# Roots pinned behind the last tanh, mLSTM sums in column groups, and keys and values spread by two rounded products

## The chip, the cores and the metric

The kernel runs on one core of a Trainium2 chip. The core has a matrix engine (TensorE, in the profile PE, with its weight loads as PEld), VectorE (DVE), ScalarE (ACT), GpSimd (POOL) and the engine that issues most DMAs (SP). Each engine takes its own instructions in order and waits on semaphores for the others. Matrix products land in PSUM, eight banks of 128 x 512 fp32; everything else lies in SBUF. The metric is the time of one execution in microseconds (us); lower is better.

## What is computed

One step of a recurrent decoder layer, for a prompt of 256 tokens and for 8 sequences of 4 new tokens, side by side: 288 columns. Three branches share one input product, their results are merged by sigmoid gates, and an MLP follows. Cut to what the change touches:

```python
proj = xn @ P['w_in']                      # then split into the branches
# RG-LRU
a = jnp.exp(log_a)
u = jnp.sqrt(-jnp.expm1(2.0 * log_a)) * (i * x)        # the roots
h = a_t * h + u_t                                      # scan over tokens
# GLA and mLSTM, for each new sequence: state update with keys and values
S = jnp.exp(bL)[..., None] * S + jnp.einsum('bhjd,bhje->bhde', k_ * jnp.exp(bL - b), v_)
C = cs[..., None, None] * C + jnp.einsum('bhj,bhjd,bhje->bhde', wj, k_, v_)
# mLSTM
S = jnp.einsum('bhid,bhjd->bhij', q_, k_) * W
den = ci * jnp.einsum('bhid,bhd->bhi', q_, n) + jnp.sum(S, axis=-1)   # the sums
# output gate of GLA
y_gla = rmsnorm(o) * jax.nn.silu(g_gate)               # the gate tanh
```

## The kernel before

**Streams.** All arrays are held with features on the 128 partitions and the 288 columns (N) free. Weights come from memory in tiles of 512 KB. `halve` (line 155 and on) splits each tile into a rounded part `hi` (ScalarE, line 164, to the type fp32r) and the remainder `lo` (VectorE, line 171). `stream_` then makes three fp32r products for each pair of a weight block and an input block (lines 197 to 199), four output blocks at a time, each in its own PSUM bank of the pool `pm` (4 banks). When a bank has its last product, `evac` empties it. A step of a stream is one weight tile: 2 x 4 x 3 = 24 products.

**Side work.** The branches' own arithmetic is written as generators (`lru`, `gla`, `gates`, `mlstm`) that `run` advances by one `yield` for each step of a stream, so that it fills the other engines while TensorE streams. The side's products take PSUM from `misc()` (pool `px`, 2 banks) or `longp()`. `run` gives them high priority and has them issued behind the current step's last product, `lo` and `hi` (`issue_after`). Within that, the order on TensorE, VectorE, ScalarE and GpSimd is made when the program is built, by a simulated run that places what is ready first; only SP's order is written out by hand. `issue_after(x)` demands a place behind x on an engine's queue; it isn't a wait.

**The roots.** `lru` starts beside the last input stage, and its 19th call falls on the first step of the merge gates, behind the two blocks of output gates (`B_GATE`). There it takes four square roots (line 759). `gate_silu` evicts a gate block: a tanh on ScalarE (line 837) and a multiply-add on VectorE (line 838). ScalarE has to load a table of functions when it goes from tanh to square root and back (ACT_TABLE_LOAD).

**The sums.** In the head loop of `mlstm`, w0 and w1 hold the weighted scores of a head for two blocks of 128 keys (256 and 128 queries wide); they lie in `e0`, in one of two places in turn. Lines 1436 and 1437 multiply them by a full 128 x 128 block of ones, which gives the sum over keys in every output row, and line 1438 copies 32 of these rows into `den`.

**Keys and values.** The new tokens' keys and values lie with (head, token) on the partitions. For the state updates they have to be spread over partitions, with a rounded part in some rows and the remainder in others, so that one fp32r product carries both. `copies` builds a selector of zeros and ones by GpSimd copies of the identity (line 862), `parts` multiplies by it in fp32 (line 876), rounds the product into `dst` (line 877), and then, with the column pairs `K_LO` and `V_LO`, turns the remainder rows into product minus rounded product (lines 881 and 882). `by_half` and `spread` follow, then `update`. The calls: `first` and `second` in `gla`, `part` in `mlstm`; 128 columns for GLA's keys, 256 for its values and for both in mLSTM. In `gla` the selector lies in slot 9, in `mlstm` in slot 4; the tile that the values later use (slot 4 in `gla`, slot 2 in `mlstm`) is taken only behind it.

Of the kernel before, what the change touches and what calls it, by code (L numbers as in the profile page):

```python
# [8 lines left out]
F32 = mybir.dt.float32  # L9
F32R = mybir.dt.float32r  # L10
# [4 lines left out]
P = 128  # L15
# [11 lines left out]
NPRE = 6  # L27


CONSTS = [("ident", 128), ("eye", 32), ("seq", 4), ("ends", 8), ("klo", 2), ("vlo", 2), ("smask", 32), ("slo", 32),  # L30
          ("glo", 128), ("causal", 128), ("bdm", 128), ("hsel", 4), ("head", 4), ("half", 2)]
PARAMS = [("bada", 96), ("g1", 16), ("lcw", 32), ("lcb", 8), ("mcw", 32), ("mcb", 8), ("ba", 8), ("bx", 8), ("lam", 8),
# [21 lines left out]
def trunk(ctx, tc, io):  # L54
# [678 lines left out]
    def lru():  # L733
        wax = slot(3)
        wa = flat(wax)[:, 0:1024].rearrange("p (n d) -> p n d", n=8)
        wx = flat(wax)[:, 1024:2048].rearrange("p (n d) -> p n d", n=8)
        G.dma_start(flat(wax)[:, 0:2048], io["lruw"])
        uc = slot(4)
        yield
        yield from conv(lx, uc, Pm("lcw"), Pm("lcb"), "lst", "o_lconv", slot(1), True)  # L740
        ls2, ls4, hb = rates
        thr, thi, tt = slot(5), slot(0), slot(1)
        aa = thr
        ps = {}
        for n in range(8 + 2):
            if n >= 2:
                i = n - 2
                for j, t in ((0, thr), (1, thi)):
                    S.activation(t[:, i, :], ps.pop((i, j))[:, :N], AF.Tanh, bias=hb[:, j, i:i + 1], scale=0.5)
                S.activation(tt[:, i, :], thr[:, i, :], AF.Tanh, bias=ls2[:, i:i + 1], scale=ls2[:, i:i + 1])  # L750
                exp = S.activation(aa[:, i, :], thr[:, i, :], AF.Exp, bias=ls4[:, i:i + 1], scale=ls4[:, i:i + 1])
            if n < 8:
                for j, w in ((0, wa), (1, wx)):
                    ps[n, j] = misc()
                    T.matmul(ps[n, j][:, :N], w[:, n, :], uc[:, n, :], start=True, stop=True)  # L755
            yield
        with tc.issue_after(exp.ins):
            for h in range(4):
                S.activation(tt[:, 2 * h:2 * h + 2], tt[:, 2 * h:2 * h + 2], AF.Sqrt, scale=-0.25)
        for h in range(4):  # L760
            r = slice(2 * h, 2 * h + 2)
            V.scalar_tensor_tensor(thi[:, r], thi[:, r], 1.0, uc[:, r], ALU.add, ALU.mult)
            V.tensor_tensor(out=thi[:, r], in0=thi[:, r], in1=tt[:, r], op=ALU.mult)
            V.scalar_tensor_tensor(thi[:, r], aa[:, r], 1.0, thi[:, r], ALU.add, ALU.mult)
            yield
        st = sc([P, 8, NB], "lh0", 1)
        V.tensor_tensor(out=st, in0=aa[:, :, NP:N:TS], in1=Pm("h0").rearrange("p (k b) -> p k b", k=8), op=ALU.mult)
        V.tensor_tensor(out=thi[:, :, NP:N:TS], in0=thi[:, :, NP:N:TS], in1=st, op=ALU.add)
        V.memset(aa[:, :, NP:N:TS], 0.0)
        V.memset(aa[:, :, 0:1], 0.0)  # L770
        hh = slot(3)
        for h in range(8):
            r = slice(h * N, (h + 1) * N)
            V.tensor_tensor_scan(flat(hh)[:, r], flat(aa)[:, r], flat(thi)[:, r], 0.0, ALU.mult, ALU.add)
            if h % 4 == 3:
                yield
        ho = sc([P, 8, 9], "lho", 1)
        G.tensor_copy(ho[:, :, 0:1], hh[:, :, NP - 1:NP])
        G.tensor_copy(ho[:, :, 1:9], hh[:, :, NP + 3:N:TS])
        G.dma_start(io["o_lh"], ho)  # L780
        ylru.extend([slot(0, F32R), slot(1, F32R)])
        for h in range(4):
            r = slice(2 * h, 2 * h + 2)
            split(ylru[0][:, r], ylru[1][:, r], hh[:, r])
            yield
# [48 lines left out]
    def gate_silu(base):  # L834
        def f(m, p):
            th = t288()
            S.activation(th, p, AF.Tanh, scale=0.5)
            V.scalar_tensor_tensor(sg[:, base + m, :], th, 1.0, p, ALU.add, ALU.mult)  # L838
        return f

# [12 lines left out]
        G.memset(qm, 0.0)  # L853
        G.tensor_copy(qm.rearrange("p n (b j) -> p n b j", b=NB)[:, :, :, 0:TS], q)

    def copies(t):

        src = ident.rearrange("p (h x g t) -> p h g x t", h=4, x=4, g=2)
        for h in range(4):
            for g in range(2):  # L860
                a = P * h + 64 * g
                G.tensor_copy(t[:, a:a + 64].rearrange("p (x r t) -> p x r t", x=4, r=4), src[:, h, g].unsqueeze(2).to_broadcast([P, 4, 4, 4]))
        return t.rearrange("p (h i) -> p h i", h=4)

    def by_head(dst, src):

# [1 line left out]
        V.tensor_tensor(out=dst, in0=src.unsqueeze(1).to_broadcast([P, 4, NS]), in1=C("head").unsqueeze(2).to_broadcast([P, 4, NS]), op=ALU.mult)  # L868
        return dst

    def parts(dst, src, rep, lo):

        n, w = dst.shape[1:]
        p = misc()[:, 0:n * w].rearrange("p (h e) -> p h e", h=n)
        for h in range(n):
            T.matmul(p[:, h], rep[:, h], src, start=True, stop=True)  # L876
        S.copy(dst, p)
        for h in range(0, n, 256 // w):
            r = slice(h, h + 256 // w)
            t = t288()[:, 0:256].rearrange("p (h e) -> p h e", e=w)  # L880
            S.activation(t, p[:, r], AF.Copy, scale=lo[:, 0:1])
            V.scalar_tensor_tensor(dst[:, r], dst[:, r].bitcast(F32), lo[:, 1:2], t, ALU.mult, ALU.add)

    K_LO, V_LO = C("klo"), C("vlo")

    def by_half(kp, other):

# [39 lines left out]
    def gla():  # L927
# [132 lines left out]
        kp = kv[:, 0:512].rearrange("p (h d) -> p h d", h=4)  # L1060
        vp = kv[:, 512:1536].rearrange("p (h e) -> p h e", h=4)
        kps = kp, kv[:, 1536:2048].rearrange("p (h d) -> p h d", h=4)
        rep = copies(bb[:, 0:512])
        yield
        sums = bb[:, 0:N]
        vx2 = flat(slot(4, F32R))[:, 0:2048].rearrange("p (i b e) -> p i b e", i=2, b=4)
        s8 = flat(slot(8))
        gn = sc([P, 2], "gn5", 1)
        V.tensor_scalar(gn, Pm("gn"), 0.5, None, ALU.mult)
# [1 line left out]
        tiles, vxs, pos = {}, {}, {}  # L1071

        def first():
            parts(kp, ks, rep, K_LO)
            parts(vp[:, 0:2], vs[:, 0:256], rep, V_LO)

        def second():
            parts(vp[:, 2:4], vs[:, 0:256], rep[:, 2:4], V_LO)
            by_half(*kps)

        def load(n):
# [209 lines left out]
    def mlstm():  # L1291
# [103 lines left out]
        nT = slot(0)  # L1395
        den = row("lf")
        cst = None
        for h in range(4):
            p = misc()
            head_bcast(p, mr, NP)(h)  # L1400
            w0, w1 = (e0[:, 384 * (h % 2) + a:384 * (h % 2) + b] for a, b in ((0, 256), (256, 384)))
            for t, w in ((0, w0), (1, w1)):
                V.tensor_scalar(w, p[:, t * P:256], col[:, t, h:h + 1], 0.0, ALU.subtract, ALU.max)
                S.activation(w, w, AF.Exp, scale=-1.0)
# [26 lines left out]
                    T.matmul(p[:, c0:e * 256 + 256], vt[:, t, h, e * P:(e + 1) * P], (w0, w1)[t],  # L1431
                             start=t == 0, stop=t == 1, skip_group_check=True)
            S.copy(nT[:, 2 * h:2 * h + 2, 0:NP], p.rearrange("p (e i) -> p e i", e=2))
            p = misc()
            r = slice(32 * h, 32 * h + 32)
            T.matmul(p[:, 0:256], ones, w0, start=True, stop=False, skip_group_check=True)
            T.matmul(p[:, 128:256], ones, w1, start=False, stop=True, skip_group_check=True)
            V.tensor_copy(den[r, 0:NP], p[r, 0:256])
            yield

        qm = slot(5)
# [3 lines left out]
        vp = kv[:, 1024:2048].rearrange("p (h e) -> p h e", h=4)  # L1445
        vn = kv[:, 2048:2056]
        V.tensor_copy(vn, C("ends"))
        rep = copies(flat(slot(4))[:, 0:512])
        pnb = sc([P, 4, 2, NB], "pnb", 1)
        s9 = flat(slot(9))  # L1450
        mn = sc([P, 2], "gn5", 1)
# [3 lines left out]
        v2 = flat(slot(2, F32R))  # L1455
        vx = v2[:, 0:1024].rearrange("p (b e) -> p b e", b=4)
        kps = kp, v2[:, 1024:2048].rearrange("p (h d) -> p h d", h=4)
        yield

        def part(dst, src, i, los):  # L1460
            parts(dst[:, 2 * i:2 * i + 2], src, rep[:, 2 * i:2 * i + 2], los)

        def ends():
            p = misc()[:, 0:64].rearrange("p (h d b) -> p h d b", h=4, d=2)
# [73 lines left out]
        def when(n):  # L1538
            return 5 + n // 2 * 3 + 2 * (n >= 10) + (n >= 14)

        do(0, part, kp, ks, 0, K_LO)
        do(0, part, vp, vs[:, 0:256], 0, V_LO)
        do(1, part, kp, ks, 1, K_LO)
        do(1, part, vp, vs[:, 0:256], 1, V_LO)
        do(2, ends)
        do(2, by_half, *kps)
        do(2, values, 0, 0)
# [189 lines left out]
def _consts():  # L1737
    import numpy as np
    p = np.arange(P)
    f = np.float32  # L1740
    c = {}
    i = np.arange(NS)
    part = p[:, None] % 16 // TS
    c["seq"] = (p[:, None] % 64) // 16 == np.arange(4)[None]
    c["ends"] = (2 * (p[:, None] % 64 // 16) + p[:, None] // 64 == np.arange(NB)[None]) & (part < 2)
    for n, lo in (("klo", part % 2 == 1), ("vlo", part >= 2)):
        c[n] = np.concatenate([lo, 1.0 - 2.0 * lo], 1)
    sm = ((p[:, None] % 32) // TS == i[None] // TS) & (p[:, None] % TS <= i[None] % TS)
    c["smask"] = sm
    c["ident"] = p[:, None] == p[None]  # L1750
    c["eye"] = p[:, None] % 32 == i[None]
    c["slo"] = np.where(sm, -BIG, 0.0)
    gm = (p[:, None] // 64 == p[None] // 64) & (p[:, None] <= p[None])
    c["glo"] = np.where(gm, -BIG, 0.0)
    c["causal"] = p[:, None] <= p[None]
    c["bdm"] = np.repeat((p[:, None] // 4 == np.arange(32)[None])[:, :, None], 4, 2).reshape(P, 128)
    c["hsel"] = p[:, None] == 32 * np.arange(4)[None]
    c["head"] = p[:, None] // 32 == np.arange(4)[None]
    c["half"] = p[:, None] // 64 == np.arange(2)[None]
    return np.concatenate([np.asarray(c[n], dtype=f) for n, _ in CONSTS], 1)  # L1760

# [91 lines left out]
```

## Time and profile before

| | us |
|---|---|
| median of 3 runs | 1941.84 (1941.18 to 1942.23) |
| profiled execution | 1942.78 |
| its span, first to last instruction | 1941.0 |
| TensorE busy in the span | 1918.4 |
| VectorE busy | 1034.7 |
| ScalarE busy | 807.8 |
| GpSimd busy | 243.5 |

The profile is of one execution, so its rows are to be set against 1942.78 and its span. A timeline row gives start, duration, engine, line, operation, what is written from what, the shape and the count of instructions merged, and in brackets how long the engine was idle before it and what ended that. Matmuls are pipelined: one of 0.29 us can follow the last after 0.13, so distances between starts say what it costs. A row of waits has the total, the number and the longest. A row of windows has its length, the busy time of each engine with the count of instructions (PE, PEld, DVE, ACT, POOL), and then the granted TensorE clock, the share of time in which the DMA engines were busy, and GB/s.

### The profile page before, as it was taken

To read this page: it belongs to the slowest core of one execution; us is meant where nothing else is said; L and a number is where in the kernel's file an instruction comes from. 1 tells how busy PE (TensorE), PEld (TensorE's weight loads), DVE (VectorE), ACT (ScalarE), POOL (GpSimd) and SP (SyncE) were. 2 spreads that over 40 slices of the span, in tenths; PEclk is the share of its full clock that TensorE was granted. 3 is DMA by queue.
4 is the path that set the end of the run, shared out by engine and by line. 5 is a ranking of instruction groups with operands and counts; after the bars stand their busy time and mean duration, and the time that the engine had idled before them with its cause. 6 is when DMAs were issued, how large, how long until landed. Compare 5 with 4: busy or idle time off the path is not lost.

```text
span 1941.0 us, 35922 instructions
## 1 busy us (share of the span) xinstructions
PE 1918.4 (99%) x15068; PEld 1829.1 (94%) x15068; DVE 1034.7 (53%) x1595; ACT 807.8 (42%) x1128; POOL 243.5 (13%) x334
## 2 busy tenths in 40 slices
PE   8999999999999999999999999999999999999997
PEld 6898989999999999899999899999999999999997
DVE  6666647545663466653454654445454444454565
ACT  4333464444454354343333454443333333333433
POOL 0000101011042112001122421000000000000101
PEclk9999999999999999999999999999999999999999
DMA  9997856557453468777788464444444445444452
GB/s 393 382 352 273 309 187 234 206 196 260 156 164 109 154 208 310 273 281 268 279 314 315 156 216 163 163 163 164 163 163 164 166 159 174 165 171 166 162 173 105
DMA packets 110066, 416.42 MB, mean 215 GB/s; under 512 B 11633, under 2 KB 11809, under 8 KB 106193
## 3 DMA queue, kind: packets, MB, share of 16 engines
q1 hardware_dynamic: 100800, 381.55, 55.1%
q0 software_dynamic: 8096, 29.19, 4.2%
q10 hardware_dynamic: 1008, 3.39, 0.5%
q8 instruction: 118, 1.93, 0.4%
q14 instruction: 44, 0.35, 0.1%
HBM read 397.27 MB, written 16.81 MB: 213 GB/s over the span
## 4 chain that ended last, share of the span: by engine, by line
PE 98%; DVE 1%; DMA 1%; SPq 0%; ACT 0%; issue 0%; DVEq 0%; ACTq 0%
PE mm L197 29%; PE mm L199 29%; PE mm L198 29%; PE pa L352 5%; DMA s<-wad 1%; PE px L1507 0%; PE px L755 0%; PE pi L1491 0%; PE px L1036 0%; PE px L1421 0%; PE px L128 0%; PE px L876 0%; PE px L1431 0%; PE mm L234 0%; PE pi L1054 0%; PE px L1109 0%
## 5 line engine op out<-in xcount | busy, mean ns | idle before, releaser
L171 DVE TENSOR_TENSOR lo<-raw,hi 128x1024 fp32r<-128x1024 f32 x448 | 549.2, 1229 | 555.1 <-ACT hi L164 531.5
L164 ACT ACTIVATE hi<-raw 128x1024 fp32r<-128x1024 f32 x444 | 470.2, 1060 | 793.5 <-PE mm L198 655.2
L197 PE MATMUL mm<-xh,hi 128*128 128x288 f32 x2528 | 747.0, 300 | 2.3 <-DVE s L838 2.3
L198 PE MATMUL mm<-xl,hi 128*128 128x288 f32 x2528 | 743.7, 296 | 0.0
L199 PE MATMUL mm<-xh,lo 128*128 128x288 f32 x2528 | 733.9, 296 | 0.7 <-DVE lo L171 0.6
L197 PEld LDWEIGHTS mm<-xh,hi 128*128 128x128 f32 x2528 | 473.0, 188 | 20.8 <-issue 11.8
L197 PE MATMUL mm<-s,hi 128*128 128x288 f32 x1664 | 491.9, 298 | 0.0
L198 PE MATMUL mm<-s,hi 128*128 128x288 f32 x1664 | 489.2, 296 | 0.0
L199 PE MATMUL mm<-s,lo 128*128 128x288 f32 x1664 | 478.8, 295 | 0.0
L198 PEld LDWEIGHTS mm<-xl,hi 128*128 128x128 f32 x2528 | 475.3, 188 | 1.3
L199 PEld LDWEIGHTS mm<-xh,lo 128*128 128x128 f32 x2528 | 472.2, 189 | 1.9 <-DVE lo L171 1.2
L197 PEld LDWEIGHTS mm<-s,hi 128*128 128x128 f32 x1664 | 312.4, 188 | 5.4 <-issue 5.0
L198 PEld LDWEIGHTS mm<-s,hi 128*128 128x128 f32 x1664 | 312.7, 188 | 0.3
L199 PEld LDWEIGHTS mm<-s,lo 128*128 128x128 f32 x1664 | 309.2, 188 | 0.2
L171 DVE TENSOR_TENSOR lo<-s,hi 128x1024 fp32r<-128x1024 f32 x80 | 98.0, 1225 | 113.4 <-ACT hi L164 113.4
L164 ACT ACTIVATE hi<-s 128x1024 fp32r<-128x1024 f32 x80 | 84.9, 1061 | 142.4 <-PE mm L198 141.7
L1681 POOL TENSOR_TENSOR t<-t 128x288 f32<-128x288 f32 x64 | 60.2, 952 | 639.2 <-ACT t L1680 639.2
L622 DVE TENSOR_TENSOR s<-s,mm 128x288 f32<-128x288 f32 x92 | 40.0, 453 | 48.3 <-PE mm L199 47.4
L1193 POOL TENSOR_TENSOR s<-s,t 128x288 f32<-128x288 f32 x32 | 36.2, 1159 | 182.1 <-DVE t L1192 182.0
L1697 DVE TENSOR_TENSOR s<-s,mm 128x288 f32<-128x288 f32 x96 | 40.3, 451 | 33.9 <-PE mm L199 32.6
L352 PE MATMUL pa<-s,silc 128*32 128x64 f32 (+3 forms) x832 | 49.8, 373 | 0.2 <-DMA s<-wad 0.2
L543 DVE TENSOR_TENSOR s<-t,s 128x288 fp32r<-128x288 f32 x64 | 33.8, 568 | 15.5 <-ACT s L542 15.5
(403 smaller groups left out, 1150.6 us busy)
## 6 DMA issues: line engine op xcount, KB each, us to landing
raw<-win SPq DMA_DIRECT2D x188, 512.0 KB, 4.3
raw<-wf SPq DMA_DIRECT2D x176, 512.0 KB, 4.1
s<-wf SPq DMA_DIRECT2D x80, 512.0 KB, 3.6
s<-wada SPq DMA_DIRECT2D x26, 1024.0 KB, 9.3
s<-wad SPq DMA_DIRECT2D x24, 1024.0 KB, 10.5
ag<-wada SPq DMA_DIRECT2D x22, 1024.0 KB, 6.0
raw<-wout SPq DMA_DIRECT2D x32, 512.0 KB, 5.3
st<-wada SPq DMA_DIRECT2D x20, 512.0 KB, 6.8
```

The lines of the kernel that those rows point to most:

```text
L164: pace["hi"] = S.activation(hi, raw, AF.Copy)
L171: pace["lo"] = V.tensor_tensor(out=lo[:, r], in0=raw[:, r], in1=hi[:, r].bitcast(F32), op=ALU.subtract)
L197: T.matmul(pss[m][:, :N], hi[:, kk, ms], xh, start=k == k0 and not take, stop=False)
L198: T.matmul(pss[m][:, :N], hi[:, kk, ms], xl, start=False, stop=False)
L199: pace["last"] = T.matmul(pss[m][:, :N], lo[:, kk, ms], xh, start=False, stop=k == kt - 1 and keep is None)
L352: pace["prod"] = T.matmul(ps[32 * j:32 * j + 32, h * w // 4:(h + 1) * w // 4], silu_c(k), v[:, j], start=k == 0 and h == 0, stop=k == KT - ...
L543: pace["mod"] = V.tensor_tensor(out=dst_l[:, r], in0=src[:, r], in1=dst_h[:, r].bitcast(F32), op=ALU.subtract)
L622: pace["adds"].append(V.tensor_tensor(out=dst[:, base + m, :], in0=dst[:, base + m, :], in1=p, op=ALU.add))
L1193: G.tensor_tensor(out=a, in0=a, in1=t, op=ALU.add)
L1681: G.tensor_tensor(out=r, in0=r, in1=r, op=ALU.mult)
L1697: V.tensor_tensor(out=a, in0=a, in1=p, op=ALU.add)
```

## The change

Three edits. The roots of `lru` get a second `issue_after`: behind the last gate tanh made so far, which `gate_silu` now records. The four heads' sums of `mlstm` are made together at the last head, by products with 32 columns of ones that go to four column groups of the array and to four ranges of PSUM partitions; for this the four heads' w0 and w1 lie in four places of `e0`. And keys and values are split ahead of the product: `parts` rounds the source (`hi`) and takes the remainder (`lo`), and multiplies both in fp32r, each with its own selector, into one sum; so `copies` builds two selectors, one for the rows that hold rounded parts and one for the remainder rows, on a zeroed tile. The selectors lie in the tile that the values use later. The scaled copies and multiply-adds behind the product, and the constants `klo` and `vlo`, go.

```diff
-        with tc.issue_after(exp.ins):
+        with tc.issue_after(exp.ins), tc.issue_after(pace["gate"].ins):
             for h in range(4):
                 S.activation(tt[:, 2 * h:2 * h + 2], tt[:, 2 * h:2 * h + 2], AF.Sqrt, scale=-0.25)
...
-            S.activation(th, p, AF.Tanh, scale=0.5)
+            pace["gate"] = S.activation(th, p, AF.Tanh, scale=0.5)
...
-    def copies(t):
+    def copies(t, lo):
 
-        src = ident.rearrange("p (h x g t) -> p h g x t", h=4, x=4, g=2)
-        for h in range(4):
+        src = ident.rearrange("p (h x g t) -> p g h x t", h=4, x=4, g=2)
+        t = t.rearrange("p (v h i) -> p v h i", v=2, h=4)
+        to = t.rearrange("p v h (g x r t) -> p v g r h x t", g=2, x=4, r=4)
+        V.memset(t.bitcast(F32), 0.0)
+        for r in range(4):
             for g in range(2):
-                a = P * h + 64 * g
-                G.tensor_copy(t[:, a:a + 64].rearrange("p (x r t) -> p x r t", x=4, r=4), src[:, h, g].unsqueeze(2).to_broadcast([P, 4, 4, 4]))
-        return t.rearrange("p (h i) -> p h i", h=4)
+                G.tensor_copy(to[:, int(r in lo), g, r], src[:, g])
+        return t
...
-    def parts(dst, src, rep, lo):
+    def parts(dst, src, reps):
 
         n, w = dst.shape[1:]
+        hi, lo = t288(F32R)[:, 0:w], t288(F32R)[:, 0:w]
+        S.copy(hi, src)
+        V.tensor_tensor(out=lo, in0=src, in1=hi.bitcast(F32), op=ALU.subtract)
         p = misc()[:, 0:n * w].rearrange("p (h e) -> p h e", h=n)
         for h in range(n):
-            T.matmul(p[:, h], rep[:, h], src, start=True, stop=True)
+            T.matmul(p[:, h], reps[:, 0, h], hi, start=True, stop=False)
+            T.matmul(p[:, h], reps[:, 1, h], lo, start=False, stop=True)
         S.copy(dst, p)
-        for h in range(0, n, 256 // w):
-            r = slice(h, h + 256 // w)
-            t = t288()[:, 0:256].rearrange("p (h e) -> p h e", e=w)
-            S.activation(t, p[:, r], AF.Copy, scale=lo[:, 0:1])
-            V.scalar_tensor_tensor(dst[:, r], dst[:, r].bitcast(F32), lo[:, 1:2], t, ALU.mult, ALU.add)
-
-    K_LO, V_LO = C("klo"), C("vlo")
+
+    K_LO, V_LO = (1, 3), (2, 3)
...
-        rep = copies(bb[:, 0:512])
+        v2 = flat(slot(4, F32R))[:, 0:2048]
+        kr, vr = copies(v2[:, 0:1024], K_LO), copies(v2[:, 1024:2048], V_LO)
         yield
...
-            w0, w1 = (e0[:, 384 * (h % 2) + a:384 * (h % 2) + b] for a, b in ((0, 256), (256, 384)))
+            w0, w1 = ws[h] = [e0[:, 384 * h + a:384 * h + b] for a, b in ((0, 256), (256, 384))]
...
-            p = misc()
-            r = slice(32 * h, 32 * h + 32)
-            T.matmul(p[:, 0:256], ones, w0, start=True, stop=False, skip_group_check=True)
-            T.matmul(p[:, 128:256], ones, w1, start=False, stop=True, skip_group_check=True)
-            V.tensor_copy(den[r, 0:NP], p[r, 0:256])
+            if h == 3:
+                p = misc()
+                for t in range(2):
+                    for i in range(4):
+                        T.matmul(p[32 * i:32 * i + 32, 128 * t:256], ones[:, 0:32], ws[i][t], start=t == 0, stop=t == 1, skip_group_check=True)
+                V.tensor_copy(den[:, 0:NP], p[:, 0:256])
             yield
...
-        rep = copies(flat(slot(4))[:, 0:512])
...
         v2 = flat(slot(2, F32R))
         vx = v2[:, 0:1024].rearrange("p (b e) -> p b e", b=4)
         kps = kp, v2[:, 1024:2048].rearrange("p (h d) -> p h d", h=4)
-        yield
-
-        def part(dst, src, i, los):
-            parts(dst[:, 2 * i:2 * i + 2], src, rep[:, 2 * i:2 * i + 2], los)
+        kr, vr = copies(v2[:, 0:1024], K_LO), copies(v2[:, 1024:2048], V_LO)
+        yield
+
+        def part(dst, src, i, reps):
+            parts(dst[:, 2 * i:2 * i + 2], src, reps[:, :, 2 * i:2 * i + 2])
```

The callers pass `kr` and `vr` in place of the selector and the column pairs.

More of the change, by code (lines that the diff above doesn't have):

```diff
@@ L27 @@
 NPRE = 6
-CONSTS = [("ident", 128), ("eye", 32), ("seq", 4), ("ends", 8), ("klo", 2), ("vlo", 2), ("smask", 32), ("slo", 32),
+CONSTS = [("ident", 128), ("eye", 32), ("seq", 4), ("ends", 8), ("smask", 32), ("slo", 32),
           ("glo", 128), ("causal", 128), ("bdm", 128), ("hsel", 4), ("head", 4), ("half", 2)]
@@ L1062, in gla @@
         kps = kp, kv[:, 1536:2048].rearrange("p (h d) -> p h d", h=4)
-        rep = copies(bb[:, 0:512])
+        v2 = flat(slot(4, F32R))[:, 0:2048]
+        kr, vr = copies(v2[:, 0:1024], K_LO), copies(v2[:, 1024:2048], V_LO)
         yield
         sums = bb[:, 0:N]
-        vx2 = flat(slot(4, F32R))[:, 0:2048].rearrange("p (i b e) -> p i b e", i=2, b=4)
+        vx2 = v2.rearrange("p (i b e) -> p i b e", i=2, b=4)
         s8 = flat(slot(8))
@@ L1073, in first @@
         def first():
-            parts(kp, ks, rep, K_LO)
-            parts(vp[:, 0:2], vs[:, 0:256], rep, V_LO)
+            parts(kp, ks, kr)
+            parts(vp[:, 0:2], vs[:, 0:256], vr)
         def second():
-            parts(vp[:, 2:4], vs[:, 0:256], rep[:, 2:4], V_LO)
+            parts(vp[:, 2:4], vs[:, 0:256], vr[:, :, 2:4])
             by_half(*kps)
@@ L1397, in mlstm @@
         cst = None
+        ws = {}
         for h in range(4):
@@ L1539, in when @@
             return 5 + n // 2 * 3 + 2 * (n >= 10) + (n >= 14)
[L1541 to L1544, printed above, removed]
+        do(0, part, kp, ks, 0, kr)
+        do(0, part, vp, vs[:, 0:256], 0, vr)
+        do(1, part, kp, ks, 1, kr)
+        do(1, part, vp, vs[:, 0:256], 1, vr)
         do(2, ends)
@@ L1745, in _consts @@
     c["ends"] = (2 * (p[:, None] % 64 // 16) + p[:, None] // 64 == np.arange(NB)[None]) & (part < 2)
-    for n, lo in (("klo", part % 2 == 1), ("vlo", part >= 2)):
-        c[n] = np.concatenate([lo, 1.0 - 2.0 * lo], 1)
     sm = ((p[:, None] % 32) // TS == i[None] // TS) & (p[:, None] % TS <= i[None] % TS)
```

## The prediction

> **What bounds the kernel now.** I read the page first, then the waits of TensorE, then the timeline at the one place where both agree that something is lost.
>
> ```profile
> span 1941.0 us, 35922 instructions
> PE 1918.4 (99%) x15068; PEld 1829.1 (94%) x15068; DVE 1034.7 (53%) x1595; ACT 807.8 (42%) x1128; POOL 243.5 (13%) x334
> ...
> PE 98%; DVE 1%; DMA 1%; SPq 0%; ACT 0%; issue 0%; DVEq 0%; ACTq 0%
> ```
>
> TensorE is busy for 99% of the span and makes 98% of the chain that ended last. So an edit is worth what it takes out of TensorE's own stream, or out of its few idle stretches; what it saves on ScalarE, VectorE or GpSimd is worth nothing unless TensorE waited for it.
>
> ```profile
> PE pi L556 <- DVE t L552: 5.9, 1, 5.9
> PE mm L197 <- DVE s L838: 2.3, 1, 2.3
> PE mm L199 <- DVE lo L171: 0.6, 1, 0.6
> ```
>
> The longest wait is at the start and the change does not touch it. The second is one wait for line 838, the second half of the SiLU eviction of the gate products. TensorE's timeline around it, and the windows of the same place:
>
> ```profile
> 272.12 0.29 PE L198 MATMUL mm<-xl,hi 128*128 128x288 f32 x1
> ...
> 277.84 0.29 PE L199 MATMUL mm<-xh,lo 128*128 128x288 f32 x1
> 280.48 0.61 PE L197 MATMUL mm<-xh,hi 128*128 128x288 f32 x1 [2.34 <-DVE s L838]
> ```
> ```profile
> 278.00:280.50 2.50, 0.16 (x2) 0.03 (x1) 2.34 (x4) 2.47 (x6) 0.00 (x0) 0.99 0.20 61
> 280.50:284.00 3.50, 3.50 (x15) 3.50 (x16) 3.22 (x6) 1.20 (x2) 0.00 (x0) 0.52 0.52 164
> ```
>
> The first two rows are 43 matmul starts apart, so one streamed matmul takes 5.72 / 43 = 0.133 us. The next was due at 277.97 and began at 280.48: 2.51 us lost. Then the granted clock (third number from the end) is 0.52 for 3.5 us, and 15 matmuls run where 3.5 / 0.133 = 26 fit: 11 x 0.133 = 1.5 us more. **The wait costs 4.0 us**, not the 2.3 that the list shows. Why line 838 was late, on ScalarE and VectorE:
>
> ```profile
> 273.48 1.28 ACT L759 ACT_TABLE_LOAD   x1
> 274.77 2.41 ACT L759 ACTIVATE s<-s 128x576 f32<-128x576 f32 x4
> 277.08 1.04 ACT L164 ACTIVATE hi<-raw 128x1024 fp32r<-128x1024 f32 x1
> 278.15 1.28 ACT L837 ACT_TABLE_LOAD   x1
> 279.44 1.01 ACT L837 ACTIVATE t<-mm 128x288 f32<-128x288 f32 x3
> ```
> ```profile
> 279.97 1.18 DVE L838 SCALAR_TENSOR_TENSOR s<-t,mm 128x288 f32<-128x288 f32 x3
> ```
>
> The four roots of line 759 and two table loads stand on ScalarE just when the last gate block's first bank is ready to be evicted. TensorE has four banks for the streams and cannot start the next block before one is free.
>
> **Part 1, the pin of the roots.** It puts the four roots and their load behind the last gate tanh. The tanh then finds its table in place and runs when its bank is done, so the wait and its slow clock go: -4.0 us. The roots then follow the last bank (277.84 plus its tail and a 0.4 us tanh), a load and 2.41 us: they end near 282.5 instead of 277.2. Queued behind them on VectorE are lines 763 and 764; the loop gives these out one quarter per stream step, so I take this delay as hidden.
>
> What is late next is the table for the following tanh. Both table loads stay; the second moves to the next function that needs it. Between the gate tanhs and line 1174 the trace has only copies on ScalarE, so it moves to the first eviction of the merge gates:
>
> ```profile
> 304.84 2.41 ACT L542 ACTIVATE s<-s 128x576 fp32r<-128x576 f32 x4 [3.62 <-DVE s L774]
> 307.15 2.00 ACT L164 ACTIVATE hi<-raw 128x1024 fp32r<-128x1024 f32 x2
> 309.05 0.98 ACT L1174 ACTIVATE s<-mm 128x288 f32<-128x288 f32 x3
> ```
> ```profile
> 309.69 0.30 PE L197 MATMUL mm<-s,hi 128*128 128x288 f32 x1
> ```
>
> ScalarE has no gap there. The first tanh starts at 309.05 and takes a third of 0.98, so its bank is free near 309.45 and TensorE takes it at 309.69: about 0.2 us to spare. A load of 1.28 us ahead of it makes a new wait of about 1.1 us. Bounds: 0 (the copies stand differently and the load fits before 304.84, where ScalarE had been idle for 3.62) and 1.1 + 1.5 (the clock falls again). I take 1.1. **Part 1 gives -2.9 us.**
>
> [...]
>
> **Part 2, the mLSTM sums.** Before, each of four heads multiplies a full block of ones by two tiles, two instructions each:
>
> ```profile
> 630.89 0.59 PE L1436 MATMUL px<-s,ones 128*128 128x256 f32 x2
> 631.32 0.39 PE L1437 MATMUL px<-s,ones 128*128 128x128 f32 x2
> 631.46 0.38 PE L197 MATMUL mm<-s,hi 128*128 128x288 f32 x1
> 631.68 0.29 PE L198 MATMUL mm<-s,hi 128*128 128x288 f32 x1
> ```
>
> From 630.89 to the next streamed matmul, 631.68 - 0.133 = 631.55, they take 0.66 us; four heads 2.6 us. After, eight products with 32 columns of ones go to four column groups at the last head. The kernel does the same in head_sums, line 909, also with fp32 and 16 instructions:
>
> ```profile
> 814.47 0.29 PE L199 MATMUL mm<-xh,lo 128*128 128x288 f32 x1
> 814.69 1.18 PE L909 MATMUL px<-s,ones 128*32 128x288 f32 x16
> 815.80 0.40 PE L197 MATMUL mm<-xh,hi 128*128 128x288 f32 x1
> 816.04 0.29 PE L198 MATMUL mm<-xl,hi 128*128 128x288 f32 x1
> ```
>
> They take 814.60 to 815.91, 1.31 us, for twice 288 columns; the new ones have 256 and 128. If all of it goes with the columns it is 1.31 x 384 / 576 = 0.87 us, if nothing does 1.31; I take 1.0, near the first. **Part 2 gives -1.6 us** (-1.3 to -1.8). The copy on VectorE becomes one in place of four.
>
> **Part 3, keys and values.** Before, every product is full fp32, two instructions each:
>
> ```profile
> 416.96 1.05 PE L876 MATMUL px<-gks,s 128*128 128x128 f32 x8
> ...
> 417.85 1.03 PE L876 MATMUL px<-vs,s 128*128 128x256 f32 x4
> ...
> 682.13 1.03 PE L876 MATMUL px<-mks,s 128*128 128x256 f32 x4
> 682.99 1.03 PE L876 MATMUL px<-vs,s 128*128 128x256 f32 x4
> ```
>
> Four with 256 columns take 0.86 us (682.13 to 682.99), 0.215 each; eight with 128 take 0.89, 0.11 each. There are 24 of the first sort (8 in GLA, 16 in mLSTM) and 8 of the second. After, the counts are the same, one for the rounded source and one for its remainder, but in fp32r. The nearest rows are the state updates, fp32r with 256 columns, and the fp32r products with 8:
>
> ```profile
> 435.04 0.74 PE L1109 MATMUL px<-s,s 128*128 128x256 f32 x4
> 435.62 0.30 PE L197 MATMUL mm<-xh,hi 128*128 128x288 f32 x1
> ...
> 692.90 0.73 PE L1467 MATMUL px<-s 128*128 128x8 f32 x6
> ```
>
> The first four take 0.58 us, 0.145 each, behind an fp32 product; scaled from the stream, 0.133 x 256 / 288 = 0.118. Between streams of their own kind I take 0.12. For 128 columns the six of 8 columns set a floor of about 0.1 (0.73 us with the last one's tail), so I take 0.11, no change. The sum is 24 x (0.215 - 0.12): **-2.3 us**. Bounds: with 0.145, -1.7; with 0.06 for the narrow ones, half of 0.12, -2.7; and if these sizes ran as fp32 does, the 24 gain nothing and the eight cost 0.215, +0.8.
>
> TensorE now also has to wait for a rounded copy on ScalarE and a subtraction on VectorE before the second product of each pair. In exchange the two scaled copies and multiply-adds behind the product go. The streamed matmuls of the step can run meanwhile, and none of the nine rows of that list of waits is of such a side chain in either branch, so I cost it at nothing. If that cover is gone it costs the chain itself, about 1 us a call.
>
> The selectors are twice as large, need two VectorE fills of 1,024 columns a branch and 16 GpSimd copies instead of 8, and they move to tiles that come free much later:
>
> ```profile
> 413.82 0.60 PE L1036 MATMUL px<-s,s 128*128 128x256 f32 x2
> ```
> ```profile
> 675.52 0.39 PE L1437 MATMUL px<-s,ones 128*128 128x128 f32 x2
> ```
> ```profile
> 667.88 1.47 POOL L862 COPY s<-con 128x64 f32<-128x64 f32 x8
> ...
> 680.62 0.53 POOL L1474 DMA_DIRECT2D st<-mC  x1 [7.31 <-DMA o_C_p<-st]
> ```
>
> In GLA the new place is the tile of the transposed values, last read at 413.82, and the spread was at 416.96; in mLSTM it is the tile of the weights, last read at 675.52, and the spread was at 682.13. At 1.47 / 8 = 0.18 us a copy, 16 take 2.9 us, plus about 1 us of fill: ready near 418.4 and 680.2. In GLA that is later than the old start, so the order must put other matmuls first, and there are streamed ones to put. The queue on GpSimd also holds the state loads; in GLA they are pushed back by those 2.9 us, and their first reader, the first head's pair, stands four stream steps of 24 x 0.133 = 3.2 us behind, which hides it. I cost it at nothing; bounds 0 and +9.4 (the slow rival below).
>
> **The sum.** -2.9 - 1.6 - 2.3 = -6.8 us. Against the profiled execution, 1942.78 us with its span of 1941.0, that is 1936.0; the median of the runs shown, 1941.84, is 0.9 lower, so I predict 1941.84 - 6.8 = **1935.0 us**.
>
> **The rivals**, each as a median:
>
> - *No new wait at the merge gates*: the load finds a gap on ScalarE. For it: ScalarE is idle for 3.62 us just before. Against it: the load follows the copies in the queue. -7.9: 1933.9.
> - *The clock falls again*: TensorE idles 1.1 us there and pays another 1.5. For it: 2.5 us of idling did so. Against it: the wait of 0.6 us in the list shows nothing like it, and 1.1 is nearer to that. -5.3: 1936.5. [...]
> - *A selector or remainder is late in one branch*: TensorE stops for some 1.5 us and the clock takes 1.5 more. For it: GLA has no slack left by the sum above. Against: the list of waits has no row for GpSimd. -3.8: 1938.0.
> - *A part does not do what it says*: fp32r of this size runs at the fp32 price (-6.8 + 2.3 + 0.8 = -3.7), or the gate eviction stays late for another reason (-6.8 + 2.9 = -3.9): about 1938.
> - *Slower*: in mLSTM the 16 copies stand behind the load at 680.62, which waits 7.31 us for a store. They start at 681.15, and with writes only four columns wide could take three times as long, 0.55 us each: ready at 690.0 for products placed at 682.1. TensorE stops for 7.9 us and loses 1.5 to the clock: -6.8 + 9.4 = +2.6, 1944.4. It decides from a delay of 5.3 us on; with as much in GLA it passes the measurement's limit. Against it: the copies are earlier in the program than the load.
>
> **How the numbers follow.** Chances: the sum as it stands 0.42, no new wait 0.12, clock again 0.12, late selector 0.18, a part without effect 0.08, slower 0.08. About 0.2% (3.9 us) is what a measurement of this kernel can tell from no change, so faster means below 1937.9. The first three lie there, 0.66; the next two straddle it, and I count 0.07 of their 0.26, which makes 0.73. Of the slow case I count 0.05 above 1945.7; the rest, 0.22, is the same. The range goes from 1932.0 (no new wait, the best of parts 2 and 3, and about a microsecond of better order) to 1940.0 (a late selector with 2 us more), which leaves out the slow case and the ends of the others, about 2 in 10.
>
> **What would show it.** Right: no wait for line 838, the clock at 1.00 between 276 and 284, four tanhs ahead of the roots, a table load at line 1174 in the first merge block with a TensorE wait of about 1 us behind it; the sums as one group of 16 within 1.0 us; the spread in groups of four within 0.5 us. Wrong: a TensorE wait on GpSimd, on the remainder, or a second stretch of half clock. Since every order on ScalarE, VectorE and GpSimd is made anew with the program, a wait at a place that I have not looked at is what would most likely make the prediction wrong.

## The result, and the profile after

The changed kernel takes 1936.17 us (median of 7 runs, 1935.36 to 1936.51), the kernel before 1941.84 (7 runs, 1941.18 to 1943.51): 5.7 us less. The ratio on record is 0.9966, with a 95% interval of 0.9957 to 0.9975, or 4.9 to 8.3 us (the two medians alone give 0.9971). In two later sets, each on one chip with its own runs of before, the difference was 7.4 and 7.3 us. The prediction was 6.8 us less.

The page of the changed kernel, the same lines as before:

```profile
span 1934.6 us, 35928 instructions
PE 1913.4 (99%) x15068; PEld 1823.9 (94%) x15068; DVE 1032.6 (53%) x1589; ACT 805.5 (42%) x1121; POOL 242.9 (13%) x350
```

Its waits of TensorE (total, times, longest):

```profile
PE pi L556 <- DVE t L552: 6.0, 1, 6.0
PE pa L352 <- DMA s<-wad: 0.6, 2, 0.5
PE mm L199 <- DVE lo L171: 0.6, 1, 0.6
```

TensorE is still busy for 99% of a shorter span. The wait for line 838 has left the list, and no other has taken its place; the one at the start has stayed, and the conditioning products' wait for a DMA (line 352), 0.2 us before, is also there, within the first 25 us. Windows around the last gate block, where the clock had been 0.52:

```profile
274.00:280.00 6.00, 5.89 (x44) 5.65 (x43) 3.26 (x6) 3.61 (x7) 0.00 (x0) 1.00 0.99 386
280.00:290.00 10.00, 10.00 (x78) 10.00 (x77) 9.59 (x14) 6.77 (x8) 0.00 (x0) 1.00 0.34 114
```

The clock stays at 1.00, and TensorE idles for 0.11 us in the window. ScalarE's timeline shows why (line 1176 is the merge gates' tanh, 1174 before):

```profile
276.40 0.40 ACT L837 ACTIVATE t<-mm 128x288 f32<-128x288 f32 x1
...
279.60 0.39 ACT L837 ACTIVATE t<-mm 128x288 f32<-128x288 f32 x1
280.01 1.28 ACT L759 ACT_TABLE_LOAD   x1
281.30 2.42 ACT L759 ACTIVATE s<-s 128x576 f32<-128x576 f32 x4
...
299.33 2.41 ACT L542 ACTIVATE s<-s 128x576 fp32r<-128x576 f32 x4 [1.25 <-DVE s L774]
301.65 1.05 ACT L164 ACTIVATE hi<-raw 128x1024 fp32r<-128x1024 f32 x1
303.47 1.06 ACT L164 ACTIVATE hi<-raw 128x1024 fp32r<-128x1024 f32 x1 [0.77 <-PE mm L198]
304.55 1.28 ACT L1176 ACT_TABLE_LOAD   x1
305.85 1.02 ACT L1176 ACTIVATE s<-mm 128x288 f32<-128x288 f32 x3
```

The first tanh runs at 276.40, the load and the roots follow the last one, and the second load has moved to the merge gates. So far it is as predicted. But TensorE's first product of the next block is due near 306.5, and the first tanh ends near 306.2: the load fits. What was left at the last gate block is on VectorE and TensorE:

```profile
276.53 1.23 DVE L171 TENSOR_TENSOR lo<-raw,hi 128x1024 fp32r<-128x1024 f32 x1 [6.03 <-ACT hi L164]
...
277.67 0.75 DVE L762 SCALAR_TENSOR_TENSOR s<-s,s 128x576 f32<-128x576 f32 x1
...
278.34 1.18 DVE L838 SCALAR_TENSOR_TENSOR s<-t,mm 128x288 f32<-128x288 f32 x3
```

The tanh was done at 276.80, but a weight remainder and a line 762 stand ahead of its multiply-add. TensorE gets the bank at 278.84 where it was due at 278.57, 0.27 us late.

Both traces hold the same 4,192 products of line 197. The difference of their start times, product by product, shows where the time goes. The columns give the change of that difference over a stretch, worked out from the traces (us); the stretches end at the given times of the trace of before and are named by what lies in them. GLA and mLSTM are the spreads of keys and values, states the updates of the mLSTM states. The first row is the change, the others are the experiments below.

```
                   to 278   to 404   to 453   to 679   to 760   to 822    later   in all
                    start    gates      GLA     sums    mLSTM   states     rest         
changed             +0.60    -3.82    -0.77    -1.61    -1.54    +0.53        0    -6.62
e1 pin              +0.52    -3.82        0        0        0    +1.13        0    -2.17
e2 sums             +0.06    -1.00        0    -1.63        0        0        0    -2.57
e3 spread           +0.81    +0.06    -0.77        0    -1.57    +1.48        0        0
e4 no pin           +0.15    +0.23    -0.77    -1.61    -1.61    +1.43        0    -2.19
e5 changed          +0.29    -3.63    -0.77    -1.61    -1.54    +0.07        0    -7.20
e6 tiles later      +0.19    -3.81    -0.77    -1.61    -1.61    -1.96    +2.71    -6.87
e7 both pins        +0.62    -2.07    -0.77    -1.61    -1.61    -1.96    +2.71    -4.70
e8 late tanh        +0.32    -3.23    -0.77    -1.61    -1.59        0        0    -6.88
e9 table early      +0.23    -3.09    -0.77    -1.61    -1.54        0        0    -6.79
e10 early alone     +0.36    -3.82    -0.77    -1.61    -1.61    +1.23        0    -6.23
e11 changed         +0.70    -3.81    -0.77    -1.61    -1.54        0        0    -7.04
```

The columns of GLA, the sums and mLSTM repeat to 0.1 us wherever the edit is in: these are the edits' own work on TensorE. The start (it varies within the first 37 us; in the trace of before the DMA engines are 0.96 busy there and TensorE's first product starts at 5.93, behind lines 552 and 554, which wait 0.28 and 0.89 us for the load of `x`) and the stretch of the states vary from profile to profile without an edit in them.

The new sums on TensorE, and one pair of each new spread, of the changed kernel (lines 881 and 882 are the two products of a pair):

```profile
669.24 0.86 PE L1441 MATMUL px<-s,ones 128*32 128x256 f32 x16
670.03 0.40 PE L197 MATMUL mm<-xh,hi 128*128 128x288 f32 x1
```
```profile
419.37 0.28 PE L881 MATMUL px<-t,s 128*128 128x128 f32 x1
419.49 0.27 PE L882 MATMUL px<-t,s 128*128 128x128 f32 x1
...
423.26 0.28 PE L882 MATMUL px<-t,s 128*128 128x256 f32 x1
423.38 0.28 PE L881 MATMUL px<-t,s 128*128 128x256 f32 x1
423.50 0.28 PE L882 MATMUL px<-t,s 128*128 128x256 f32 x1
```

Starts are 0.12 us apart for 256 columns and 0.11 for 128, both as assumed. The sums take 0.9 us with the step to the next streamed product.

### The profile page after: what moved, and what is told of

Its sections match the earlier page's. It is cut to its first block, busy times and chain, and to the rows that moved or that the text cites. A ratio compares the mean times of both kernels' runs of the same rounds, so it can differ in the third digit from the quotient of the medians.

```text
span 1934.6 us, 35928 instructions
## 1 busy us (share of the span) xinstructions
PE 1913.4 (99%) x15068; PEld 1823.9 (94%) x15068; DVE 1032.6 (53%) x1589; ACT 805.5 (42%) x1121; POOL 242.9 (13%) x350
## 4 chain that ended last, share of the span: by engine, by line
PE 97%; DMA 2%; DVE 1%; ACT 0%; issue 0%; SPq 0%; DVEq 0%; ACTq 0%
PE mm L197 29%; PE mm L199 28%; PE mm L198 28%; PE pa L352 4%; DMA raw<-win 1%; DMA s<-wad 1%; PE px L755 0%; DMA s<-x 0%; PE px L1511 0%; PE px L1037 0%; PE px L1424 0%; PE px L128 0%; PE pi L1495 0%; PE px L1434 0%; PE pi L1055 0%; PE pi L490 0%
```

## The experiments

All times are medians. The kernel before had 1942.89 us beside e1 to e4, 1943.31 beside e5 to e8 and 1943.28 beside e9 to e11.

### e1: the pin alone

```diff
-        with tc.issue_after(exp.ins):
+        with tc.issue_after(exp.ins), tc.issue_after(pace["gate"].ins):
```

> The kernel before with the pin of the roots alone. If the wait of TensorE and the slow clock behind it are what the pin removes, the stretch around 278 us loses 3.6 to 4.0 us (2.5 of idling and 1.5 of half clock, less some 0.3 us that VectorE still holds back), the clock stays at 1.00, and the time falls by 3.6 to 4.0. If a new wait of 1.1 us at the first merge gates appears without the other two edits, it falls by 2.5 to 2.9. If the wait goes only because the other edits shift the order, it stays and the time is the same.

1939.68 us, 0.9985 of before (0.9976 to 0.9993): 3.2 us less, somewhat under the 3.6 to 4.0 expected. The gates' stretch lost 3.82 us and the clock stayed at 1.00, so the pin alone does all that the changed kernel shows there, and no wait appeared at the merge gates. In the states' stretch this profile gave 1.13 back.

### e2: the sums alone

```diff
-            T.matmul(p[:, 0:256], ones, w0, start=True, stop=False, skip_group_check=True)
-            T.matmul(p[:, 128:256], ones, w1, start=False, stop=True, skip_group_check=True)
+            if h == 3:
...
+                        T.matmul(p[32 * i:32 * i + 32, 128 * t:256], ones[:, 0:32], ws[i][t], start=t == 0, stop=t == 1, skip_group_check=True)
```

> The kernel before with the sums in column groups alone. Theory: TensorE's stream gets 1.6 us shorter between 628 and 676 us and nothing else moves; the wait for line 838 and the half clock at 280 stay. Rival: the products in column groups are late for the copy or for the next head's weights, and less than 1 us is left at the end.

1941.24 us, 0.9993 (0.9984 to 1.0002): 1.65 less in the medians, which alone is not clear of noise, and 1.63 on TensorE in the sums' stretch. The wait for line 838 was there with its 2.3 us, but the windows (as above) show no slow clock behind it. Those of e4, which has the same wait, do:

```profile
280.00:288.00 8.00, 7.46 (x56) 7.46 (x57) 6.14 (x11) 2.04 (x5) 0.00 (x0) 1.00 0.39 131
```
```profile
280.00:288.00 8.00, 7.38 (x44) 7.38 (x45) 6.23 (x11) 1.84 (x4) 0.00 (x0) 0.79 0.38 131
```

e2 runs 56 products in this window, e4 44. (e2's stretch of the gates is shorter by only 1.00: 1.54 from the clock, and 0.5 lost again where a tanh of the merge gates is late.) So the same wait is not followed by a slow clock every time: it was in before, e3 and e4, and not in e2. The last section shows how the stops of these profiles lie.

### e3: the two rounded products alone

```diff
-            T.matmul(p[:, h], rep[:, h], src, start=True, stop=True)
+            T.matmul(p[:, h], reps[:, 0, h], hi, start=True, stop=False)
+            T.matmul(p[:, h], reps[:, 1, h], lo, start=False, stop=True)
```

> The kernel before with the two rounded products alone. Theory: 0.77 us less in the GLA branch and 1.54 in the mLSTM branch, 2.3 in all, no wait of TensorE for the selectors. Rival: without the sums in one burst the selectors' tile in mLSTM comes free at another moment, GpSimd's copies come late, and TensorE idles there for 1 us or more, so that 1.5 or less is left.

1941.61 us, 0.9995 (0.9987 to 1.0004): 1.3 less, not clear of noise by itself. TensorE's own work fell by 0.77 and 1.57, 2.34, and no selector was late. The profile lost 1.48 of it in one wait of the state products for a state tile:

```profile
PE pi L1493 <- DMA s<-mC: 1.4, 1, 1.4
```

### e4: without the pin

> The changed kernel without the pin. If the three parts add up, the time lies 3.9 us below before and 3.6 to 4.0 above the changed kernel's value in the same set, with the 2.3 us wait and the half clock back near 278 us. If they do not add up, the difference to before is not the sum of the other two runs (1.6 and 2.3) within 0.5.

1940.06 us, 0.9987 (0.9978 to 0.9995): 2.8 less, where e2 and e3 give 1.65 + 1.28 = 2.9. With e1's 3.2 that makes 6.0 to 6.1, within the 5.7 to 7.4 of the changed kernel, which had no runs in this set. Each of these differences is uncertain by more than 1 us; that the parts add up is shown by the columns of the table, where GLA, sums and mLSTM have the values of e2 and e3 and the gates' 3.8 us are missing. The wait and the half clock were back. Here it was the weight remainder that was late near 800 us, behind the weights themselves; the waits of that stretch (740 to 812 us):

```profile
ACT hi L164 <- DMA raw<-win: 17.0, 5, 8.0
...
PE mm L199 <- DVE lo L171: 0.7, 1, 0.7
```

### e5 and e11: the changed kernel again

> The changed kernel once more, for comparison with the next two on one chip. The three edits alone gave 3.2, 1.7 and 1.3 us against the median of before; if they add up, 5.5 to 6.5 us below before. TensorE's timeline should again be shorter by 1.63 us in the sums, 0.77 in the GLA spread and 1.54 in the mLSTM spread; what differs from look to look is the first 37 us and the stretch from 770 to 805 us.

> The changed kernel a third time, as the measure for the two above: 5.7 to 7.4 us below before, as in the two sets so far; on TensorE's timeline 3.8 us less at the gates, 0.77 and 1.54 in the spreads, 1.63 in the sums.

1935.95 us, 0.9962 (0.9950 to 0.9975), and 1936.00, 0.9965 (0.9952 to 0.9977): 7.4 and 7.3 less. The first is more than the 5.5 to 6.5 that had been expected from the three edits alone. The changed kernel's runs stay within 1.6 us (1935.36 to 1936.94 over all), those of before spread over 4.6 (1941.18 to 1945.77).

### e6: the conditioning tiles later

```diff
-    every("L L . V . . .", skip=5)
+    every("L L . V . . .", skip=10)
```

> The changed kernel with the two conditioning tiles of 1 MB, which SP issues near 777 us, sent five stream steps later. Theory: between 740 and 812 us the DMA engines are the limit (0.9 busy), the weight tiles of the output-gate blocks are queued behind these 2 MB, and TensorE's wait for the remainder near 800 us (0.5 to 1.1 us in the looks so far) goes: 0.5 to 1.0 us less than the changed kernel. Rival: the weights are late because their buffers come free late, or the tiles pay the same time later; then it is the same within 0.3.

1936.33 us, 0.9965 (0.9951 to 0.9979): the same as e5 within 0.4. The waits of ScalarE for weights from 740 to 812 us, in e5 and here:

```profile
ACT hi L164 <- DMA raw<-win: 21.9, 8, 7.5
```
```profile
ACT hi L164 <- DMA raw<-win: 2.4, 1, 2.4
```

So the weights are late there because of these 2 MB, which confirms that half of the theory. The other half was not put to the test: in e5 TensorE had no wait in that stretch that could go. The conditioning products that went from the stretch (-1.96) cost 2.71 later, and nothing is won.

### e7: line 762 pinned as well

On top of e6:

```diff
+            pace["silu"] = V.scalar_tensor_tensor(sg[:, base + m, :], th, 1.0, p, ALU.add, ALU.mult)
...
+            with tc.issue_after(pace["silu"].ins):
                 V.scalar_tensor_tensor(thi[:, r], thi[:, r], 1.0, uc[:, r], ALU.add, ALU.mult)
```

> As the run before, and line 762 on VectorE also pinned behind the last gate eviction. Theory: in the changed kernel VectorE runs one weight remainder (1.23 us) and one line 762 (0.75) before the first eviction of the last gate block and TensorE waits 0.27 us for the bank; without line 762 there the wait goes, 0.3 us less than the run before. Rival: the wait stays, because the remainder in front takes the bank past its time anyway.

1938.68 us, 0.9978 (0.9969 to 0.9987): 2.35 us slower than e6, where 0.3 less had been expected. The 0.27 at the last gate block went (4.10 less there), but a wait came up at the merge gates. ScalarE's timeline and the wait (line 1177 is the tanh):

```profile
302.15 2.41 ACT L542 ACTIVATE s<-s 128x576 fp32r<-128x576 f32 x4 [4.42 <-DVE s L775]
304.46 1.99 ACT L164 ACTIVATE hi<-raw 128x1024 fp32r<-128x1024 f32 x2
306.47 1.28 ACT L1177 ACT_TABLE_LOAD   x1
307.77 1.01 ACT L1177 ACTIVATE s<-mm 128x288 f32<-128x288 f32 x3
```
```profile
PE mm L197 <- ACT s L1177: 1.9, 1, 1.9
```

This is the queue that the prediction drew: four copies, two roundings without a gap, the load, the tanh. The block is due at 306.20, so the copies start 4.05 us ahead of it, in the changed kernel 7.23, and in the trace of before, from which the prediction took its 1.1 us, 4.85. The clock stayed at 1.00:

```profile
306.00:309.00 3.00, 1.13 (x9) 0.89 (x7) 2.18 (x2) 2.97 (x6) 2.70 (x3) 1.00 0.28 67
309.00:315.00 6.00, 6.00 (x49) 5.78 (x51) 1.97 (x2) 2.33 (x4) 0.90 (x2) 1.00 0.90 281
```

### e8: a later tanh

```diff
+                if br == 0 and b == 0 and m == 0:
+                    idle = t288()
+                    for _ in range(3):
+                        S.activation(idle, p, AF.Copy)
                 S.activation(gt[:, m, :], p, AF.Tanh, scale=0.5)
```

> The changed kernel with three copies of 0.4 us on ScalarE in front of the first tanh of the merge gates, behind the table load. If only about 0.2 us of slack is left there, as the prediction had it for a load of 1.28 us, TensorE stops for about 1.0 us at 306 us. If the roots' pin has made more room than 1.2 us, it does not stop. And if an idle stretch of about 1 us is enough for the clock to fall, a half clock of 3.4 us follows and costs 1.5 more; if not, the clock stays at 1.00.

1936.19 us in a single run. The copies read the bank and so wait for it. Two of the three came ahead of the load and the third behind the first tanh, which was 0.7 us later, not 1.2. TensorE waited:

```profile
PE mm L197 <- ACT s L1181: 0.3, 1, 0.3
```

From the starts, TensorE stopped for 0.49 us, so about 0.25 us of room was left behind the load in the changed kernel. The clock stayed at 1.00.

### e9 and e10: the table loaded early

```diff
+            with tc.issue_after(root.ins):
+                S.activation(sc([P, 1], "warm", 1), eps, AF.Tanh)
```

e9 with line 762 pinned, e10 with this alone; neither has e6's edit.

> The changed kernel with line 762 pinned on VectorE as in the run of both pins (the conditioning tiles stay where they were), and a tanh of one column right behind the last root, so that the table of the merge gates is loaded near 283 us, where ScalarE is idle. Theory: the 2.0 us wait at the merge gates in the run of both pins is the table load and nothing else; with the load out of the way there is no wait there, and with 0.3 us less at the last gate block the time is 0.3 us below the changed kernel of this set. Rival: the wait stays at 0.7 us or more because the four copies of line 542 come late by themselves.

> The changed kernel with the early tanh alone. Theory: its table load is hidden already, so the time stays within 0.3 us of the changed kernel of this set, and the only difference is the room ahead of the first tanh of the merge gates, 1.3 us more. Rival: the load costs TensorE something there that the list of waits does not show, and 0.5 us or more is gained.

e9: 1936.83 us, 0.9968 (0.9955 to 0.9980), 0.8 above the changed kernel of its set. The load left the merge gates, and the wait of 1.9 shrank, but not to nothing:

```profile
301.98 2.41 ACT L542 ACTIVATE s<-s 128x576 fp32r<-128x576 f32 x4 [4.64 <-DVE s L777]
304.29 1.99 ACT L164 ACTIVATE hi<-raw 128x1024 fp32r<-128x1024 f32 x2
306.19 0.99 ACT L1179 ACTIVATE s<-mm 128x288 f32<-128x288 f32 x3
```
```profile
PE mm L197 <- ACT s L1179: 0.5, 1, 0.5
```

From the starts TensorE stops for 0.61 us where it stopped for 2.03 in e7: about 1.4 us of that were the load, and the rest is the four copies, which are late with line 762 pinned (4.0 us ahead of the block, as in e7). So the load was the greater part of that wait, not the whole of it. e10: 1935.87 us, 0.9963 (0.9950 to 0.9977), as the changed kernel (1936.00): there the load is hidden, as its timeline showed. None of these beats the changed kernel.

## Why the prediction was right, and where it was not

**Part 2 and part 3 held.** The sums were put at -1.6 and are -1.61 to -1.63 in every profile that has them. The spread was put at -2.3 and is -0.77 - 1.54 = -2.31 (to -2.38). Both came from the starts of the nearest instructions in the trace, not from the durations in the page's groups (a pipelined matmul's 0.38 us would have given about twice the price).

**The wait for line 838.** It was put at 4.0 us with its slow clock, and the pin took 3.82, all by itself (e1). With the wait wholly gone it is 4.10 (e7); the 0.27 that the pin leaves are line 762 and a remainder on VectorE ahead of the eviction. The prediction looked at ScalarE's queue only. That the slow clock comes each time was wrong: e2 has the wait without it. So of the 4.0, 2.5 are there in every profile with the wait and 1.5 are paid in some executions. How often shows in the mean granted clock of each run. In the profiles it is 0.9967 to 0.9973 with the slow stretch and 0.9976 to 0.9982 without. Of the 57 runs of before beside the experiments, 36 have 0.997 (median 1943.5 us) and 21 have 0.998 (median 1941.8). So it comes in rather more than half of the executions; the count is rough, since 4 of the 17 runs of the changed kernel read 0.997 too.

**The new wait at the merge gates is the step that failed.** The prediction took 1.1 us for the table load that moves there. The load did move, line and place, but it costs nothing. The sum took the place of the copies of line 542 from the trace of before and moved only the load. In fact those copies wait for the last of the eight scans of line 774 on VectorE, and the scans were ordered anew too. Before:

```profile
297.30 1.23 DVE L171 TENSOR_TENSOR lo<-raw,hi 128x1024 fp32r<-128x1024 f32 x1 [1.32 <-ACT hi L164]
...
299.40 3.31 DVE L774 TENSOR_TENSOR_SCAN s<-s,s 128x288 f32<-128x288 f32 x5
...
302.75 2.06 DVE L774 TENSOR_TENSOR_SCAN s<-s,s 128x288 f32<-128x288 f32 x3
```

After:

```profile
294.01 5.29 DVE L774 TENSOR_TENSOR_SCAN s<-s,s 128x288 f32<-128x288 f32 x8
```

The next block is due at 309.69 and 306.56, and the last scan ends at 304.81 and 299.30: 4.9 us ahead of it before, 7.3 after. These 2.4 us take up the load of 1.28 and a wait of 0.77 of the second rounding for TensorE, with about 0.25 left over (e8). e7 shows the mechanism itself: with the copies late, the load sits in front of the tanh and TensorE stops for 2.0 us. That is 0.9 more than the 1.1 of the prediction, and the copies stand 0.8 closer to the block than before. So the price was right for a place that the copies did not keep. Why the scans come earlier is only in part the order: in the trace of before the remainder ahead of them also waits 1.32 us for a rounding whose weights were late, and in the changed kernel 0.21. The runs do not separate the two.

**Slow clock again, a late selector, parts without effect: none came.** The selectors came near to it. GpSimd's copies in mLSTM, of the changed kernel:

```profile
671.48 1.49 POOL L864 CAST s<-con 128x64 fp32r<-128x64 f32 x8 [4.11 <-DVE s L861]
678.16 0.53 POOL L1478 DMA_DIRECT2D st<-mC  x1 [5.19 <-DMA o_C_p<-st]
678.69 1.57 POOL L864 CAST s<-con 128x64 fp32r<-128x64 f32 x8
```

The second selector did stand behind the state load that waits for a store, as the slow rival had it; but a copy took 0.2 us, not 0.55. The selector was ready at 680.26, and the first product of line 881 or 882 behind that starts at 681.13.

**What the sum did not have.** Without the new wait it comes to -7.7 by the measured terms (-3.82 - 1.61 - 2.31). The first comparison gave 5.7, the later ones 7.3 and 7.4: the changed kernel's median stays at 1936.0 to 1936.2, that of before moves from 1941.8 to 1943.3. The slow clock accounts for most of this. The prediction took the 4.0 us from a profile that has the slow clock (1942.78 us) and subtracted them from a median of three runs that by their times most likely had none (1941.18 to 1942.23). Of the seven runs of the first comparison, five lie there too. Against an execution without the slow clock the 1.5 us are not there to be won, and the measured terms come to -6.2. The clock of these seven runs is not on record, so this is argued from their times, not shown.

The stretch of the states, too, takes back 0 to 1.5 us in one profile or another (0.53, 0.07 and 0 in the three of the changed kernel). There the DMA engines are 0.9 busy (the number before the last, window of the changed kernel):

```profile
740.00:770.00 30.00, 30.00 (x243) 28.31 (x242) 18.93 (x40) 11.42 (x15) 7.74 (x12) 1.00 0.90 327
```

What sets this loss in one execution was not found; before has 0.91 in the same window. The 6.8 lies between the results, and in part by luck: a wait too many made up for two things left out.

## What to carry to other kernels

Price a wait of the bounding engine with what follows it, but look at more than one profile before the slow clock behind it is counted as certain, and subtract a price from times of executions that paid it. When an instruction is moved, everything that the planner orders by readiness moves with it: a place in a queue read from the old trace holds only for what is tied to it. And where a stretch varies by 1.5 us between executions, as the states do here, a gain of that size is read from the stretch that the edit touches, not from the total of one profile.

## What the runs showed of the hardware

A stop of TensorE of about 2.5 us was followed by 3.4 us of half clock in before, e3 and e4 and by none in e2; the 2.0 us in e7 had none. The traces record when the granted clock changes. In before it first rises 10.80 us after the first instruction; the half clock begins 269.653 us behind that rise and lasts 3.412, and the fall behind the last product comes 1921.703 us behind it. In the changed kernel the first rise is at 10.89, and the one fall, again behind the last product, comes 1914.877 us behind it. With 269.653 / 79 as a step (3.4133 us, the half clock's own length within 2 ns), the other two distances are 563 and 561 steps within 4 ns; in e4 the half clock starts 79 steps behind the first rise too, in e3 80. Steps of this length, counted in each profile from its own first rise and laid over the stops, give, in us (worked out from the traces; idle time runs from the recorded end of one product to the start of the next):

```
          TensorE idle        idle in each step it touches     clock in the next step
before    278.13 to 280.48    2.32, 0.02                       half
e3        278.94 to 281.28    2.34                             half
e4        278.28 to 280.62    2.34                             half
e2        278.19 to 280.54    0.95, 1.39                       full
e7        306.36 to 308.23    0.64, 1.23                       full
e3        768.66 to 770.06    1.40                             full
```

The wait for line 838 lies in one step in before (but for 0.02 us), e3 and e4, and the next step ran at half clock; in e2 a boundary divides it, and the next ran at full clock. Among these six stops, a step with 2.3 of its 3.41 us idle was followed by half clock and a step with 1.4 or less was not; none lies between. The step in before was not wholly idle: 3.41 - 2.32 leaves 1.1 us of products. No experiment moved a stop against the steps, so this is what the profiles have in common, not a tested cause.
